# A two-layer encoder: x of the first MLP kept in DRAM tile by tile, 16 adaLN vectors computed in the space it leaves, and the squares and splits of the projection put in another order

## The chip, the cores and the metric

The kernel runs on one core of a Trainium2 chip. The metric is device time in microseconds (us). Three runs of the kernel before took 2743.26, 2744.90 and 2745.24 us; the median is 2744.9.

The engines have short names in the profile: PE is TensorE (matrix products), PEld its loads of the stationary operand, DVE is VectorE, ACT is ScalarE, POOL is GpSimd, and SPq is the queue on which SyncE issues transfers. A few transfers are issued from ACT's queue.

## The reference

All in float32, for one sequence of 1024 positions with 1024 features:

```python
cond = silu(c)
for i in range(2):
    mod = cond @ ada_w[i] + ada_b[i]                # 6 x 1024 numbers
    sh1, sc1, g1, sh2, sc2, g2 = split(mod, 6)
    h = rmsnorm(x, norm1_g[i]) * (1 + sc1) + sh1
    y = gqa_attention(h, ...) if i == 0 else chunked_gmlp(h, ...)
    x = x + g1 * y
    h = rmsnorm(x, norm2_g[i]) * (1 + sc2) + sh2
    x = x + g2 * (square(relu(h @ mlp_w_in[i])) @ mlp_w_out[i])
```

Layer 0 mixes with attention (16 heads, 4 key-value heads, QK norm and rotary positions), layer 1 with a gated unit of 3072 channels (gMLP). The MLPs have 4096 hidden features. An adaLN "vector" below is 128 of the 12 x 1024 numbers in `mod`: a tile of 128 x 1024 weights, each row multiplied by `cond` and summed. There are 96 of them. They are named (layer, j, k): j from 0 to 5 says which of shift, scale and gate, k from 0 to 7 which 128 features.

## The kernel before

x is kept transposed, as 16 tiles of 128 features by 512 positions: `x[hf][k]`, hf the half of the positions, k the block of features. Products are made in float32 precision from pairs: an operand is split into a rounded part `hi` (a cast on ACT) and a remainder `lo` (a subtraction, mostly on DVE; `split`, L285, and the last lines of each `prep`), and three matmuls hi·hi, hi·lo, lo·hi stand for one. The large products use one level of Winograd's scheme: seven products of half-size blocks in place of eight, named "1" to "7", with sums and differences of blocks ahead of them and of results behind them.

The stages in order, with their part of the profiled span: the projection to q, k and v (0 to about 205 us), attention, the output projection of attention (`wo_mm`, to 679), the first product of the first MLP (`winograd`, 112 units of 12 matmuls, 679 to 1004.6), its second product (`Out`, 112 units, to 1334), the values of the gMLP (`wino_v`), its other half (`winograd`, 84 units), its output product (`Out`, 84 units, 1854 to 2105), and the two products of the second MLP, to the end. `Out` reads the hidden activations from DRAM, where the first product has put them as ready-made forms: `load_f` (L1035) loads a form, `split_f` splits it (L287, L288), `prep` splits a weight block (L1057, L1058), `take` and `add` (L1089) add a result times the gate to x. `spread` makes the forms (L1141 to L1144), and SP stores them (L1145, L1146).

Between the products run hooks, called after each unit `i`: `at(i)` in the first product, `at_out(i)` in the second. They put the work of a norm, of a store or of a vector at a chosen unit. The numbers at the end of the file (HB, MO, MG and others) are these places.

Vectors are made in four ways and places. For those that the projection needs, `first_h` calls `mod_load`. `Slabs` makes 32 on POOL during attention. `mods(n)` takes the next n of the list `pending` (48 at the start) and is called in the projection, at the end of attention and in the output projection. The last 16 of the list, (1, 3, k) and (1, 5, k), are left for two later places: 12 are made in the second product of the first MLP, one at every third unit from unit 14 (`MO = (14, 3, 1)`), 4 in the output product of the gMLP, one at every fourth unit from unit 16 (`MG = (16, 4, 1)`). `mod_load` loads 128 x 1024 weights (L141), multiplies and sums on DVE (L145, followed by a short read of the accumulator) and adds the bias (L148). In both places the condition vector is loaded anew, spread over 128 partitions (`load_cond`, L134), and SiLU is applied to it (L137). These tiles come from a part of memory with the tag "c", four tiles of 128 x 1024, which `cut(4)` sets up 6 units before the first vector.

x stays in its 16 tiles (tag "x") through the whole first MLP. For the gMLP it is spilled: `spill` (L1279) stores each half in DRAM, since the gMLP needs the tiles, and `load_xs` (L1525) brings it back in four portions in the output product.

The order of work on each engine and queue is not that of the text alone. A planner takes the instructions in the order of the text, with the waits that their data and their tiles give, and lets a later instruction pass an earlier one when it reckons that the later one can start first. `pin` forbids this for one instruction: it stays behind everything that the text has before it on its engine. The multiplies of `mod_load` are pinned, and so is the SiLU (L137). The resulting order of each engine is fixed when the program is built; nothing is reordered while it runs, and a queue whose next transfer must wait holds back all that are behind it.

In the projection, `qkv_w(cb, kp, eng)` loads two tiles of weights and splits them: the casts on ACT (L498), the remainders on `eng` (L499), which is POOL (`G`) or DVE (`V`). `SquareSum.add` squares a tile on ACT (L231) and adds it to a running sum on DVE (L235). `norm_rstd` makes the norm's factor of it: a small product for the row sums (L244), a root, and a product that spreads the factor over the partitions (L255).

## Time and profile before

| | |
|---|---|
| median of three runs | 2744.9 us |
| time of the profiled execution | 2744.76 us |
| its span, first to last instruction | 2742.9 us |
| mean granted clock of TensorE | 0.984 |
| PE busy | 96% of the span, 12804 matmuls |
| DVE busy | 83%, 3191 instructions |
| ACT busy | 53%, 2598 instructions |
| POOL busy | 39%, 716 instructions |
| DMA | 427.52 MB, 156 GB/s on average |

A busy PE is not a PE at its peak: matmuls overlap, so the durations of single ones add up to more than the time that they take, and at a lower granted clock PE is busy and slow. How many matmuls fall into a stretch of time says more than its busy share. In rows of a timeline, a bracket with an arrow at the end gives the idle time of the engine ahead of the instruction and what ended it. The view of waits gives, for each pair of a waiting line and a releasing line, the total, the number and the longest wait.

### The profile page before, as it was taken

The page shows a single profiled execution, that of the slowest core. Times are in us where ns is not written, and L with a number is a line of the kernel's source. Part 1 is how long each engine was busy: PE and PEld are TensorE (multiplying, and loading weights), DVE is VectorE, ACT ScalarE, POOL GpSimd, SP SyncE. Part 2 cuts the span into 40 slices and gives each one's busy share as a digit, 9 for nine tenths or more (in the row PEclk, how much of TensorE's full clock was granted, in tenths as well). Part 3 has the DMA queues.
Part 4 walks back from the last instruction along what each step waited for, and adds up shares of the span by engine and source line. Part 5 has one row for each costly group of instructions (what it writes and reads, how often), then busy time and mean ns, then how long its engine had stood idle before and what let it go on. Part 6 is the DMA issues. An engine that isn't in the chain of part 4 may idle for free. (4 is left out here: it accounts for less than half of the span.)

```text
span 2742.9 us, 37309 instructions
## 1 busy us (share of the span) xinstructions
PE 2642.3 (96%) x12804; PEld 2184.9 (80%) x12804; DVE 2275.4 (83%) x3191; ACT 1454.5 (53%) x2598; POOL 1063.8 (39%) x716
## 2 busy tenths in 40 slices
PE   7889999999899999999999999999989999999999
PEld 5668999887688887777778888887868688878877
DVE  7889888888887778998797777787998887789993
ACT  4448999964644455435443355444436554554442
POOL 2448777534300024451543255556541400034520
PEclk9999999999999999999999999999999999999999
DMA  7241111225164458826244345558642364478462
GB/s 263 71 138 47 62 55 55 80 95 182 66 210 151 160 205 313 293 81 206 79 134 131 108 166 180 181 189 315 234 131 66 111 205 149 162 260 287 142 203 70
DMA packets 200544, 427.52 MB, mean 156 GB/s; under 512 B 23137, under 2 KB 35425, under 8 KB 200354
## 3 DMA queue, kind: packets, MB, share of 16 engines
q1 hardware_dynamic: 173474, 387.37, 41.6%
q10 hardware_dynamic: 26880, 37.76, 3.7%
q8 instruction: 101, 1.65, 0.2%
q14 instruction: 89, 0.73, 0.1%
HBM read 306.56 MB, written 118.49 MB: 155 GB/s over the span
## 5 line engine op out<-in xcount | busy, mean ns | idle before, releaser
L1074 PE MATMUL out<-t,s 128*128 128x512 f32 x1232 | 487.0, 396 | 14.3 <-DVE t L288 14.3
L1073 PE MATMUL out<-t,s 128*128 128x512 f32 x1232 | 487.0, 396 | 6.8 <-ACT t L287 6.8
L1075 PE MATMUL out<-t,s 128*128 128x512 f32 x1232 | 485.8, 395 | 6.0 <-DVE s L1058 5.7
L415 PE MATMUL w<-t,s 128*128 128x512 f32 x1168 | 460.1, 395 | 0.5 <-ACT t L287 0.5
L416 PE MATMUL w<-t,s 128*128 128x512 f32 x1168 | 455.5, 391 | 1.5 <-DVE t L288 1.1
L417 PE MATMUL w<-t,s 128*128 128x512 f32 x1168 | 454.9, 389 | 0.9 <-DVE s L401 0.9
L288 DVE TENSOR_TENSOR t<-t,t 128x512 fp32r<-128x512 f32 x408 | 377.9, 940 | 28.7 <-ACT t L287 21.2
L287 ACT CAST t<-t 128x512 fp32r<-128x512 f32 x408 | 244.3, 617 | 157.9 <-DMA t<-hf 65.2
L400 ACT CAST s<-w 128x512 fp32r<-128x512 f32 x292 | 174.3, 619 | 229.7 <-PE w L417 164.1
L1074 PEld LDWEIGHTS out<-t,s 128*128 128x128 f32 x1232 | 234.9, 191 | 70.7 <-DVE t L288 21.3
L1073 PEld LDWEIGHTS out<-t,s 128*128 128x128 f32 x1232 | 234.4, 190 | 60.1 <-ACT t L287 11.0
L1075 PEld LDWEIGHTS out<-t,s 128*128 128x128 f32 x1232 | 234.8, 191 | 59.3 <-DVE s L1058 11.1
L401 DVE TENSOR_TENSOR s<-w,s 128x512 fp32r<-128x512 f32 x292 | 227.9, 789 | 59.0 <-ACT s L400 55.4
L1044 POOL TENSOR_TENSOR w<-w,t 128x512 f32<-128x512 f32 x32 | 53.0, 1658 | 557.2 <-DMA t<-in_wm_dram 279.3
L416 PEld LDWEIGHTS w<-t,s 128*128 128x128 f32 x1168 | 219.4, 188 | 51.0 <-DVE t L288 6.7
L415 PEld LDWEIGHTS w<-t,s 128*128 128x128 f32 x1168 | 219.2, 188 | 49.6 <-issue 3.4
L417 PEld LDWEIGHTS w<-t,s 128*128 128x128 f32 x1168 | 219.3, 188 | 46.4 <-DVE s L401 1.3
L1058 DVE TENSOR_TENSOR s<-t,s 128x512 fp32r<-128x512 f32 x240 | 212.2, 886 | 49.2 <-ACT s L1057 46.4
L1057 ACT CAST s<-t 128x512 fp32r<-128x512 f32 x240 | 147.6, 620 | 188.7 <-PE out L1075 115.6
L860 DVE TENSOR_TENSOR t<-t,t 128x512 fp32r<-128x512 f32 x256 | 164.3, 683 | 20.9 <-ACT t L854 20.9
L837 DVE TENSOR_REDUCE mx<-s 128x1 f32<-128x1024 f32 x128 | 156.6, 1224 | 23.7 <-PE s L834 22.4
L870 PE MATMUL o<-t,t 128*128 128x256 f32 x1024 | 163.7, 293 | 0.0
(247 smaller groups left out, 5438.1 us busy)
## 6 DMA issues: line engine op xcount, KB each, us to landing
t<-hf SPq DMA_DIRECT2D x320, 256.0 KB, 4.5
hf<-c SPq DMA_DIRECT2D x156, 256.0 KB, 2.1
w<-in_wi_dram SPq DMA_DIRECT2D x64, 512.0 KB, 4.3
hf<-c ACTq DMA_DIRECT2D x96, 256.0 KB, 2.0
c<-in_ada_dram SPq DMA_DIRECT2D x36, 512.0 KB, 4.7
w<-in_adan_dram SPq DMA_DIRECT2D x32, 512.0 KB, 3.3
t<-in_wm_dram SPq DMA_DIRECT2D x64, 256.0 KB, 5.3
wf<-w SPq DMA_DIRECT2D x64, 256.0 KB, 3.3
```

Source lines behind the costliest of these rows:

```text
L287: S.copy(hi, src)
L288: (eng or V).tensor_tensor(lo, src, f32(hi), ALU.subtract)
L400: S.copy(hi, src)
L401: V.tensor_tensor(lo, src, f32(hi), ALU.subtract)
L415: T.matmul(ps, hi[:, a], th, start=kt == 0, stop=False)
L416: T.matmul(ps, hi[:, a], tl, start=False, stop=False)
L417: T.matmul(ps, lo[:, a], th, start=False, stop=kt == 3)
L860: pin(V.tensor_tensor(lo, pt, f32(hi), ALU.subtract))
L1058: V.tensor_tensor(lo, src, f32(hi), ALU.subtract)
L1073: T.matmul(ps, hi[:, a], th, start=begin and kt == 0, stop=False)
L1074: T.matmul(ps, hi[:, a], tl, start=False, stop=False)
L1075: T.matmul(ps, lo[:, a], th, start=False, stop=end and kt == 3)
```

## The change

1. **x of the first MLP through DRAM.** In the first product, at units 14 to 29 (HB + 12 and on), `spill` stores the 16 tiles of x in DRAM, one per unit. In the second product `load_xs` brings them back in four portions of four tiles: before the first unit, and at units 2, 6 and 10, as the gMLP does in its output product. `spill` takes a list of tiles now, and `xd`, `spill`, `load_xs` and the table of places XL have moved ahead of `mlp`. The gMLP's own spill stays.
2. **The last 16 vectors in the space left.** A new class, `Halves`, makes them in the first product of the first MLP out of free x tiles of 128 x 512: at unit 30 the condition vector is loaded as two halves, at unit 34 SiLU is applied to each and the weights of two vectors are loaded, as two halves each, and from unit 42 on, at every fourth unit (MX = 4), a vector is made by two multiplies with sums, one per half, while the next is loaded. The sums of both halves stay in a small tile, and when 8 vectors are done two short instructions add the halves and the bias for all 8 (before, one short instruction per vector). Neither the multiplies nor the SiLU is pinned.
3. **Vectors leave the second products.** The calls of `mods`, `load_cond` and `silu_cond` in `at_out` of the MLP and of the gMLP are gone. `cut(4)` is made at unit 8 in both (CUT = 8); it was at 8 in the MLPs and at 10 in the gMLP.
4. **The projection.** Three calls of `qkv_w` make their remainders on DVE in place of POOL (six subtractions), and the squares and sums of the second half of x, so far all eight in one loop, are added in three portions: tiles 0 to 2, 3 to 5, and 6 to 7, at three places.

```diff
--- before.py
+++ after.py
@@ -128,13 +128,6 @@
     ng = const.tile([P, 2, 2, KT], F32, name="ng")
     amod = const.tile([P, 2, 2, KT], F32, name="amod")
     cond = []
-
-    def load_cond(tile_):
-        cond[:] = [tile_]
-        nc.sync.dma_start(tile_, t["cond"].broadcast_to([P, D]))
-
-    def silu_cond():
-        pin(S.activation(cond[0], cond[0], AF.Silu))
 
     def mod_load(layer, j, k, tag="w", late=True):
         raw = wide(tag)
@@ -691,16 +684,20 @@
 
         ps = banks(True)
         kk = k_split(kd)
-        qkv_w(2, 1, G)
+        qkv_w(2, 1, V)
         qkv_mm(2, 0, ps, hs)
         r1 = q_copies(pq)
+        for k in range(3):
+            sq1.add(xs1[k])
         rr = q_sums(r1)
-        qkv_w(2, 2, G)
+        qkv_w(2, 2, V)
         qkv_mm(2, 1, ps, hs)
+        for k in range(3, 6):
+            sq1.add(xs1[k])
         q_rope(0, 1, r1, rr, (0, 1))
-        for k in range(KT):
+        qkv_w(2, 3, V)
+        for k in range(6, KT):
             sq1.add(xs1[k])
-        qkv_w(2, 3, G)
         qkv_mm(2, 2, ps, hs)
         rb1 = norm_rstd(sq1, bank_x)
         q_rope(0, 1, r1, rr, (2, 3))
@@ -1151,6 +1148,57 @@
     def forms_dram(n):
         return [{q: dram.tile([P, 512], F32, name=nm("hf")) for q in OUT_FORMS} for _ in range(n)]
 
+
+    xd = [[dram.tile([P, 512], F32, name=nm("xd")) for _ in range(KT)] for _ in range(2)]
+
+    def spill(hf, ks=range(KT)):
+        for k in ks:
+            nc.sync.dma_start(xd[hf][k], x[hf][k])
+
+    def load_xs(hf, odd):
+        for k in range(odd, KT, 2):
+            x[hf][k] = xslot()
+            nc.sync.dma_start(x[hf][k], xd[hf][k])
+
+    XL = {-1: (0, 0), 2: (0, 1), 6: (1, 0), 10: (1, 1)}
+
+
+    class Halves:
+        def __init__(self, todo):
+            self.todo, self.raw, self.part = list(todo), [], {}
+
+        def start(self):
+            self.cond = [xslot(), xslot()]
+            for h in range(2):
+                nc.sync.dma_start(self.cond[h], t["cond"][:, h * 512 : (h + 1) * 512].broadcast_to([P, 512]))
+
+        def silu(self):
+            for h in range(2):
+                S.activation(self.cond[h], self.cond[h], AF.Silu)
+
+        def load(self):
+            if self.todo:
+                layer, j, k = self.todo.pop(0)
+                raw = [xslot(), xslot()]
+                for h in range(2):
+                    nc.sync.dma_start(raw[h], t["ada"][layer, j * KT + k][:, h * 512 : (h + 1) * 512])
+                self.raw.append((layer, j, k, raw))
+
+        def step(self):
+            if not self.raw:
+                return
+            layer, j, k, raw = self.raw.pop(0)
+            self.load()
+            if k == 0:
+                self.part[j] = small.tile([P, 2, KT], F32, tag="half", name=nm("half"), bufs=2)
+            part = self.part[j]
+            for h in range(2):
+                V.scalar_tensor_tensor(raw[h], raw[h], 1.0, self.cond[h], ALU.mult, ALU.mult,
+                                       accum_out=part[:, h, k : k + 1])
+            if k == KT - 1:
+                V.tensor_tensor(part[:, 0], part[:, 0], part[:, 1], ALU.add)
+                V.tensor_tensor(mod[:, layer, j], part[:, 0], adab[:, layer, j], ALU.add)
+
     def mlp(layer, f, sqB, done, hook):
         hidden = forms_dram(16)
         out_ = Out(t["wm"][layer], hidden, 4, mod[:, layer, 5])
@@ -1177,9 +1225,22 @@
 
         n = 16 * 7
         rest = []
+        halves = None if layer else Halves(pending)
 
         def at(i):
             more(f, RW, None)
+            if halves:
+                h = i - HB - 12
+                if 0 <= h < 2 * KT:
+                    spill(h // KT, (h % KT,))
+                elif h == 2 * KT:
+                    halves.start()
+                elif h == 2 * KT + 4:
+                    halves.silu()
+                    halves.load()
+                    halves.load()
+                elif h > 2 * KT + 8 and h % MX == 0:
+                    halves.step()
             if i == HB:
                 rest.append(norm_ss(sqB, bank_y))
             elif i == HB + 1:
@@ -1195,17 +1256,15 @@
             stores.pop(0)()
 
         def at_out(i):
-            if i == MO[0] - 6:
+            if i == CUT:
                 cut(4)
-                if pending:
-                    load_cond(cwide())
-            elif pending and i == MO[0] - 2:
-                silu_cond()
-            if len(pending) > 4 and i >= MO[0] and (i - MO[0]) % MO[1] < MO[2]:
-                mods(1, "c")
+            if halves and i in XL:
+                load_xs(*XL[i])
             if hook and i >= out_.n - out_.tail:
                 hook(i - out_.n + out_.tail)
 
+        if halves:
+            load_xs(*XL[-1])
         out_.run(at_out, done)
 
     wo_sums(1)
@@ -1270,13 +1329,8 @@
         else:
             pieces[ct] = ((2 * i + 1, 0, P),)
 
-    xd = [[dram.tile([P, 512], F32, name=nm("xd")) for _ in range(KT)] for _ in range(2)]
     vd = [[dram.tile([2, P, 2, 256], F32, name=nm("vd")) for _ in range(4)] for _ in range(6)]
     st = small.tile([P, 8, 6, 6], F32, tag="st", name="st", bufs=1)
-
-    def spill(hf):
-        for k in range(KT):
-            nc.sync.dma_start(xd[hf][k], x[hf][k])
 
     def wino_v(f, hook):
 
@@ -1519,22 +1573,11 @@
         upto(n + 9)
         while stores:
             stores.pop(0)()
-        def load_xs(hf, odd):
-            for k in range(odd, KT, 2):
-                x[hf][k] = xslot()
-                nc.sync.dma_start(x[hf][k], xd[hf][k])
-
-        load_xs(0, 0)
-        XL = {2: (0, 1), 6: (1, 0), 10: (1, 1)}
+        load_xs(*XL[-1])
 
         def at_out(i):
-            if i == MG[0] - 6:
+            if i == CUT:
                 cut(4)
-                load_cond(cwide())
-            elif pending and i == MG[0] - 2:
-                silu_cond()
-            if pending and i >= MG[0] and (i - MG[0]) % MG[1] < MG[2]:
-                mods(1, "c")
             if i in XL:
                 load_xs(*XL[i])
             if i >= out_.n - out_.tail:
@@ -1565,8 +1608,8 @@
 FA = 3
 LO = 3
 TG = ((0, 0), (1, 0), (1, 1), (0, 1))
-MO = (14, 3, 1)
-MG = (16, 4, 1)
+CUT = 8
+MX = 4
 LW = 5
 IG = 30
 SW = 3
```

## The prediction

> **What bounds the kernel now.** I read the page first, then the busy times by stage, then the waits of PE, the instruction groups of the two stages the change takes work from, and the order of SP's queue.
>
> ```profile
> span 2742.9 us, 37309 instructions
> PE 2642.3 (96%) x12804; PEld 2184.9 (80%) x12804; DVE 2275.4 (83%) x3191; ACT 1454.5 (53%) x2598; POOL 1063.8 (39%) x716
> ```
>
> Each of the 12804 matmuls must be issued, and PE is idle for only 100.6 us of the span. An edit can win what PE loses in pauses and at a reduced clock, and can lose by adding pauses. The profiled execution took 2744.76 us, 1.86 us more than its span and 0.14 us under the median of the three runs, 2744.9; the sum below is made against 2744.76 and needs no shift.
>
> The next view cuts the span into stretches: length, then busy time and count of each engine, the granted clock PEclk, DMA share and GB/s.
>
> ```profile
> 70.00:120.00 50.00, 39.47 (x164) 30.20 (x164) 38.94 (x68) 20.02 (x41) 27.20 (x18) 0.86 0.20 65
> 679.00:764.00 85.00, 75.16 (x294) 57.32 (x293) 72.32 (x97) 46.59 (x83) 37.74 (x24) 0.92 0.25 84
> 764.00:1004.60 240.60, 240.60 (x1063) 199.31 (x1062) 185.70 (x293) 122.63 (x210) 0.00 (x0) 1.00 0.51 180
> 1004.60:1044.00 39.40, 36.13 (x149) 28.53 (x148) 31.83 (x35) 21.10 (x38) 24.47 (x16) 0.96 0.72 259
> 1044.00:1199.00 155.00, 153.70 (x673) 125.49 (x672) 152.28 (x196) 65.12 (x114) 78.33 (x49) 1.00 0.70 244
> 1199.00:1254.00 55.00, 48.74 (x188) 37.28 (x187) 52.51 (x65) 24.91 (x45) 23.31 (x15) 0.91 0.47 154
> 1889.00:1994.00 105.00, 105.00 (x464) 86.95 (x464) 104.22 (x121) 48.47 (x85) 61.79 (x39) 1.00 0.76 273
> 1994.00:2054.00 60.00, 52.98 (x203) 40.84 (x201) 56.07 (x67) 25.54 (x46) 23.62 (x16) 0.89 0.40 126
> 2425.50:2480.00 54.50, 52.88 (x232) 42.78 (x231) 47.37 (x53) 29.76 (x54) 27.77 (x17) 1.00 0.79 289
> 2480.00:2610.00 130.00, 130.00 (x575) 107.67 (x574) 123.96 (x147) 59.13 (x105) 70.95 (x45) 1.00 0.60 198
> 2610.00:2742.90 132.90, 126.01 (x545) 102.86 (x544) 85.81 (x121) 42.34 (x74) 16.56 (x11) 0.99 0.41 139
> ```
>
> 679 to 1004.6 is the first product of the first MLP, 1004.6 to 1334 its second product, 1854 to 2105 the output product of the gMLP, 2425.5 to the end the second product of the last MLP. In 764:1004.6 PE never pauses: 240.6 us over 1063 matmuls is 0.2263 us each, the price without loss. At that price: 679:764 loses 18.5 us (85 less 294 x 0.2263); in the first MLP's second product the three stretches lose 5.7, 2.7 and 12.5; the gMLP's output product loses 14.1 in 1994:2054; the last product 2.0, nothing and 9.6. In each of the late losses VectorE (DVE) has just been full: 152.28 of 155 us in 1044:1199, 104.22 of 105 in 1889:1994.
>
> **The change, part by part.**
>
> **Vectors leave the two output products.** The groups of 1004.6:1334, then those of 1854:2105 (busy us, mean ns | idle before):
>
> ```profile
> L1089 DVE SCALAR_TENSOR_TENSOR x<-t,mod,x 128x512 f32<-128x512 f32 x16 | 18.9, 1192 | 0.0
> L145 DVE SCALAR_TENSOR_TENSOR c<-c,c 128x1024 f32<-128x1024 f32 x12 | 16.8, 1403 | 0.0
> L148 DVE TENSOR_TENSOR mod<-mod,adab 128x1 f32<-128x1 f32 x12 | 5.0, 414 | 0.0
> L145 DVE DVE_READ_ACCUMULATOR c<-c,c 128x1 f32 x12 | 0.9, 77 | 0.0
> ```
>
> ```profile
> L145 DVE SCALAR_TENSOR_TENSOR c<-c,c 128x1024 f32<-128x1024 f32 x4 | 6.7, 1667 | 0.0
> L148 DVE TENSOR_TENSOR mod<-mod,adab 128x1 f32<-128x1 f32 x4 | 1.6, 392 | 0.0
> ```
>
> In the first MLP's second product 12 vectors go: 16.8 + 5.0 + 0.9 = 22.7 us of DVE; in the gMLP's output product 4, 6.7 + 1.6 and a third of those 0.9, 8.6. Their 16 transfers, two loads of the condition vector and two SiLUs go from there too. What is late without them? SP's queue shows it, in order of time and then in its waits (total, times, longest):
>
> ```profile
> 1168.24 4.41 SPq L1035 DMA_DIRECT2D t<-hf  x3
> 1198.73 0.32 SPq L1279 DMA_DIRECT2D xd<-x  x1
> 1199.14 0.38 SPq L1035 DMA_DIRECT2D t<-hf  x1
> ```
>
> ```profile
> SPq L1279 <- DVE x L1089: 107.1, 16, 26.1
> ```
>
> The spill of x for the gMLP (L1279), which the program text has behind this product, stands inside it: the planner puts a transfer where it thinks the data are ready. DVE, behind by then, wrote x (L1089) late, SP stood still for 26.1 us at the longest, and the loads of activations behind it (L1035) started at 1199.14. PE paused there, as it had before, for other loads:
>
> ```profile
> 1202.49 0.50 PE L1073 MATMUL out<-t,s 128*128 128x512 f32 x1 [1.10 <-ACT t L287]
> ```
>
> ```profile
> 1031.67 0.51 PE L1073 MATMUL out<-t,s 128*128 128x512 f32 x1 [1.51 <-ACT t L287]
> 1033.00 0.51 PE L1074 MATMUL out<-t,s 128*128 128x512 f32 x1 [0.82 <-DVE t L288]
> ```
>
> So the 2.7 + 12.5 = 15.2 us lost after 1044 come from DVE's lag through that spill. The spill stays; the lag shrinks. Bounds: 0 (the spill waits anyway) and 15.2. The nearest row is the last product, the same 112 units without vectors, whose stores of the output wait for the same x: DVE is at 123.96 of 130 us and the stretch behind loses 9.6, of which 4 lie after the last matmul's start:
>
> ```profile
> 2738.82 0.39 PE L1075 MATMUL out<-t,s 128*128 128x512 f32 x1
> ```
>
> I take 15.2 - 5.6 = about **10 us**. The early 5.7 us, before the first vector, stay. For the gMLP's output product the bounds are 0 and 14.1; I take **4**, in proportion to the DVE time (8.6 against 22.7). Moving the cut from unit 10 to 8 there only renames free memory: nothing, or the wait for a tile if one is still in use.
>
> The clock belongs to this. With pauses of 1.51 and 0.82 us and matmuls between them, the next 5 us were granted 0.66:
>
> ```profile
> 1034.00:1039.00 5.00, 5.00 (x16) 3.91 (x15) 3.70 (x5) 2.38 (x5) 3.34 (x2) 0.66 1.04 394
> ```
>
> In the Trainium skill, "TensorE: Matmul & The Clock Gate", Part 1, the array falls to half rate after at least one idle window of about 3.4 us; by that rule pauses as short as these cost no clock, 1199:1254 would give back at most its idle 55 - 48.74 = 6.3 us, the 10 would be about 5 and the sum 5 us higher. The row shows a fall after shorter pauses, so I price it by the row.
>
> **The vectors in the first product.** Added: 32 multiply-and-sum over 128x512 with 32 accumulator reads and 4 short adds. The nearest price is that of L1089, one input in PSUM and no POOL beside it:
>
> ```profile
> L1089 DVE SCALAR_TENSOR_TENSOR x<-out,mod,x x124: 735/742/752, 1022.2 to 2739.2; 128x512 f32<-128x512 f32 x124
> ```
>
> At its median of 0.74 and the 0.08 of an accumulator read above that is 26 us. The text puts them at units 42 to 102, inside 764:1004.6, where DVE has 240.6 - 185.70 = 54.9 us free and POOL does nothing: hidden there. The cover is not certain. The multiplies are not pinned to the text's order, as those of before were, so the planner can move them ahead, as it moved the spill, into 679:764, where DVE is at 72.32 of 85 and PE already loses 18.5. Ends: 0 when all are covered, 26 when all are ahead of needed work; less than nothing is excluded, since nothing leaves DVE here. I take **4**, nearer to the covered end: a planner that fills gaps finds most of them in the longer stretch.
>
> The Trainium skill, "SBUF — State Buffer", Who interferes with whom, says that a DVE instruction with two SBUF inputs contends with a GpSimd instruction reading SBUF. The trace agrees: x<-t,mod,x takes 1192 ns on average beside POOL above, x<-out,mod,x, with one input in PSUM, 742.
>
> **x through DRAM.** Added on SP: 16 spills, 16 reloads, and 32 half loads plus 2 for the condition, in place of 16 and 2 of double size.
>
> ```profile
> c<-in_ada_dram SPq DMA_DIRECT2D x36, 512.0 KB, 4.7
> xd<-x SPq DMA_DIRECT2D x16, 256.0 KB, 2.0
> x<-xd SPq DMA_DIRECT2D x16, 256.0 KB, 5.5
> ```
>
> A transfer itself lies beside matmuls (DMA is at 0.51 in 764:1004.6), and reloads of 5.5 us have the whole of that stretch free for them: nothing, and if that is gone a reload holds an x add and, through it, DVE. The condition's halves wait for two x tiles that a spill has left, a half load for a tile that a multiply has read; behind them on SP stand the product's weights and the stores of the hidden forms, which wait for DVE at the same place. The gMLP's own spill waits for the reloads of the same buffers, long done: nothing. What can cost is order on SP: a spill moved ahead to where x is just being written makes the weight loads behind it wait, as L1279 did. Ends: 0, and the 12.5 us of 1199:1254, the one place where such a spill went wrong. I take **1**: these x are final before the stage begins, so few can meet an unfinished one. SiLU moves with its table load to ScalarE at 122.63 of 240.6 us: nothing.
>
> **The projection.** Six lo-splits go from POOL to DVE, and the squares of the second half of x are summed in three portions. DVE, POOL and PE in order of time:
>
> ```profile
> 72.94 1.29 DVE L499 TENSOR_TENSOR t<-c,t 128x512 fp32r<-128x512 f32 x2
> 82.44 2.67 DVE L605 TENSOR_TENSOR t<-t,t 128x512 fp32r<-128x512 f32 x4 [1.88 <-ACT t L604]
> 87.52 2.47 DVE L557 TENSOR_REDUCE qss<-t 128x8 f32<-128x512 f32 x4 [2.40 <-ACT t L556]
> 96.06 9.59 DVE L235 TENSOR_TENSOR t<-t,t 128x512 f32<-128x512 f32 x7
> ```
>
> ```profile
> 100.12 3.39 POOL L499 TENSOR_TENSOR t<-c,t 128x512 fp32r<-128x512 f32 x2
> ```
>
> ```profile
> 101.89 0.58 PE L510 MATMUL qkv<-t,t 128*128 128x512 f32 x1 [4.44 <-POOL t L499]
> 105.71 1.87 PE L244 MATMUL ss<-ones,t 128*128 128x1 f32 x8 [1.97 <-DVE t L235]
> 118.40 0.50 PE L509 MATMUL qkv<-s,t 128*128 128x512 f32 x1 [0.23 <-ACT t L268]
> ```
>
> PE waits 4.44 us for POOL's split and 1.97 for the row sum behind seven adds that take 9.59 us, 1.37 each, beside POOL. The first matmul on the new half starts at 118.40, 12.7 after that sum. Without POOL's splits an add costs what a DVE split costs, 1.29 / 2 = 0.65: seven adds and six splits are 8.4 us, and 1.88 + 2.40 of idle time (rows 82.44 and 87.52) can take some. Added to the 96.06 at which DVE now begins its adds, the last ends between 100.2 and 104.5, 5.4 to 1.2 us before 105.65. Ends: a gain of 10.5 (PE's loss there: its idle time in 70:120, 50 - 39.47), and a loss of 3.9, six DVE splits in front of the rest of the chain. I take **5**, the upper part of that 1.2 to 5.4, as the pause at 101.89 and the clock behind it (0.86 in 70:120) go with it.
>
> Sum: 2744.76 - 10 - 4 + 4 + 1 - 5 = 2730.76, **2731 us**; all costs at the ends taken alone: 2744.76 - 15.2 - 14.1 - 10.5 = 2705 and 2744.76 + 26 + 12.5 + 3.9 = 2787.
>
> **The rivals.**
>
> **The vectors arrive early and DVE's full stretch grows** (slower). Place: 679:764. Price: up to 26 us for multiplies and up to 12.5 for spills that hold weights, against the 4 + 1 in the sum: 2731 + 33.5 = 2764 at the worst. It decides when the cost passes the 10 + 4 + 5 = 19 us won elsewhere, that is when some 23 of the 32 multiplies stand in front of work that PE waits for. For it: 18.5 us already lost there, and the spill's place in SP's row. Against: DVE is idle for 12.7 of these 85 us, too, and the planner gives way to earlier work when both are ready.
>
> **The gain of the output products does not come** (no change). The spill L1279 and loads behind it remain, and other work fills DVE: in 2480:2610, without vectors, it is at 95%. Then only the projection's 5 and the costs of 5 are left: 2745. Against: with DVE that full there PE loses nothing in that stretch.
>
> **DVE becomes the bound in the projection.** The six splits come before the sums that PE waits for: instead of 5 won, 3.9 lost: 2740, at the edge of no change. For it: DVE is at 38.94 of 50 us in 70:120. Against: POOL slowed it there, and leaves.
>
> **How the numbers follow.** No change means within 0.2%, 5.5 us, about what a measurement can tell. The forecast, with its own range 2714 to 2739, 0.66; DVE in the projection 0.06, half of it faster and half no change; the gain that does not come 0.08; the early vectors 0.20. So faster 0.69, same 0.11, slower 0.20. The range reaches up into the early vectors, to 2757, and down to 2714, where both output products give nearly all they lose.
>
> **What would show it.** In the profile after: no L145 rows beyond the first product, DVE under 90% in the stretch that now reads 152.28 of 155, SP's wait at L1279 well under 26.1, the pause at 1202 gone and the clock 1.00 there; the sum of squares done by 104 us; and DVE rows of the halves mostly behind the first 85 us of the MLP. Wrong if these rows stand in those 85 us and the stage is longer than 325.6 us by over 15, or if L1279 still holds SP for 20 us, or if new x reloads or spills head SP's waits.

## The result, and the profile after

The changed kernel takes 2745.5 us (median of 20 runs, 2742.0 to 2752.3) against 2744.4 us for the kernel before (20 runs, 2740.7 to 2748.2): ratio 1.0005, 95% interval 0.9998 to 1.0012. Nothing was won. The forecast was 2731 us and faster.

The profiled execution of the changed kernel took 2751.21 us, 5.7 us over its own median, and the one of before 2744.76, 0.36 over its. So the two traces differ by 6.45 us, more than the medians do, and a length of one stage read from one trace is good to some 3 or 4 us: stages that the change does not touch differ by that much between the kernels below (the values product of the gMLP took 241.6 to 245.4 us, the attention 393.8 to 397.4).

Cut at the first matmul of each stage, in us:

| stage | before | after | difference | forecast |
|---|---|---|---|---|
| projection | 185.7 | 181.3 | -4.4 | -5 |
| attention | 396.3 | 396.3 | 0 | 0 |
| attention output | 97.0 | 99.5 | +2.5 | 0 |
| first MLP, first product | 325.7 | 343.1 | **+17.4** | +5 |
| first MLP, second product | 329.0 | 320.5 | -8.5 | -10 |
| gMLP, values | 242.4 | 245.4 | +3.0 | 0 |
| gMLP, u | 281.2 | 281.1 | -0.1 | 0 |
| gMLP, output product | 252.6 | 249.5 | -3.1 | -4 |
| last MLP, both products and what follows | 634.9 | 634.5 | -0.4 | 0 |

The three gains came, nearly as large as forecast. One stage gave all of it back. The page's first lines after, then the busy times by stretch (columns as before: stretch, length, busy time and count of PE, PEld, DVE, ACT, POOL, then PEclk, DMA share, GB/s), each stretch lying in its stage within some 3 us of where the one of before lay:

```profile
span 2749.4 us, 37427 instructions
PE 2639.9 (96%) x12804; PEld 2183.9 (79%) x12804; DVE 2269.4 (83%) x3217; ACT 1452.0 (53%) x2597; POOL 1050.8 (38%) x710
```

```profile
70.00:120.00 50.00, 42.57 (x188) 32.60 (x187) 42.42 (x81) 23.33 (x45) 20.01 (x12) 0.93 0.21 70
677.00:762.00 85.00, 62.62 (x219) 44.16 (x217) 80.08 (x145) 42.36 (x74) 31.71 (x20) 0.84 0.60 194
762.00:1020.00 258.00, 258.00 (x1137) 213.43 (x1138) 197.83 (x311) 131.62 (x224) 5.08 (x4) 1.00 0.53 181
1020.00:1060.00 40.00, 38.17 (x159) 30.56 (x158) 35.85 (x36) 21.39 (x39) 25.67 (x16) 0.96 0.76 277
1060.00:1215.00 155.00, 155.00 (x685) 128.40 (x684) 140.88 (x169) 66.97 (x119) 77.55 (x50) 1.00 0.61 204
1215.00:1270.00 55.00, 49.83 (x209) 39.24 (x209) 51.59 (x72) 23.68 (x43) 20.76 (x13) 0.97 0.47 163
1902.00:2007.00 105.00, 105.00 (x462) 86.89 (x461) 96.26 (x110) 46.48 (x82) 59.08 (x38) 1.00 0.69 243
2007.00:2067.00 60.00, 53.82 (x227) 42.54 (x226) 56.21 (x76) 26.43 (x49) 23.08 (x15) 0.97 0.42 132
```

At the forecast's price of a matmul without loss, 0.2263 us, 677:762 loses 85 - 219 x 0.2263 = 35.4 us, where before it lost 18.5. The rest of the stage is without loss, as before (258.00 of 258). The second product loses 4.0, nothing and 7.7, where before it lost 5.7, 2.7 and 12.5; the gMLP's output product 8.6 where it lost 14.1, behind a stretch in which VectorE (DVE) is at 96.26 of 105 us (before 104.22). PE's and DVE's totals on the page hardly move, so the time is a matter of when, not of how much.

In 677:762 DVE is now at 80.08 of 85 us with 145 instructions, against 72.32 with 97. The new ones are the multiplies with their reads, 26.57 us in this stretch. All 32 ran between 665.5 and 745 us, not at units 42 to 102 where the text has them (line's own view: shortest, median, longest in ns, then first and last start):

```profile
L1196 DVE SCALAR_TENSOR_TENSOR x<-x,x x32: 665/686/1785, 665.5 to 743.3; 128x512 f32<-128x512 f32 x32
L1196 DVE DVE_READ_ACCUMULATOR x<-x,x x32: 76/80/89, 666.1 to 745.0; 128x1 f32 x32
```

What PE waited for in that stretch, before and then after (total, times, longest):

```profile
PE w L415 <- ACT t L287: 4.4, 3, 2.6
PE w L417 <- DVE t L288: 4.1, 3, 1.6
```

```profile
PE w L408 <- ACT t L280: 12.1, 4, 9.1
PE w L409 <- DVE t L281: 5.6, 5, 1.7
PE w L410 <- DVE t L281: 4.2, 4, 2.4
```

The longest of these, 9.1 us, reads as a chain when the engines are set in order of time. PE, then the same 9 us as a stretch, then ACT and SP:

```profile
692.35 0.79 PE L408 MATMUL w<-t,t 128*128 128x512 f32 x1 [9.08 <-ACT t L280]
```

```profile
683.28:692.35 9.07, 0.00 (x0) 0.00 (x0) 9.07 (x17) 2.25 (x5) 3.22 (x2) 0.75 0.53 158
```

```profile
687.75 0.63 ACT L224 ACTIVATE t<-x 128x512 f32<-128x512 f32 x1 [4.93 <-DVE x L793]
691.68 1.28 ACT L280 CAST t<-t 128x512 fp32r<-128x512 f32 x2 [2.31 <-DMA t<-in_wi_dram]
```

```profile
681.29 6.12 SPq L1184 DMA_DIRECT2D x<-in_ada_dram  x3
687.50 1.81 SPq L360 DMA_DIRECT2D t<-in_wi_dram  x4
```

```profile
673.87 3.81 SPq L367 DMA_DIRECT2D t<-in_wi_dram  x8
```

While PE did nothing for 9.07 us, DVE was busy for all 9.07. ScalarE stood 4.93 us for an update of x that DVE (L793) was late with, and then 2.31 us for a weight load. That load (L360, a small weight tile of forms 1 or 2) was issued at 687.50, behind half loads (L1184) that stood in SP's queue from 681.29. Before, all eight such loads had gone out in one row from 673.87. The chain has two possible roots, DVE's time and SP's order, and this trace alone does not part them.

### The profile page after: what moved, and what is told of

Read it like the earlier page. It is cut to its first block, busy times and chain, and to the rows that moved or that the text cites. A ratio compares the mean times of both kernels' runs of the same rounds, so it can differ in the third digit from the quotient of the medians.

```text
span 2749.4 us, 37427 instructions
## 1 busy us (share of the span) xinstructions
PE 2639.9 (96%) x12804; PEld 2183.9 (79%) x12804; DVE 2269.4 (83%) x3217; ACT 1452.0 (53%) x2597; POOL 1050.8 (38%) x710
## 5 line engine op out<-in xcount | busy, mean ns | idle before, releaser
L1071 PEld LDWEIGHTS out<-t,s 128*128 128x128 f32 x1232 | 233.5, 190 | 65.9 <-DVE t L281 17.4
```

The source lines that it names most:

```text
L1071: T.matmul(ps, hi[:, a], tl, start=False, stop=False)
```

## The experiments

Theory V: the early multiplies take DVE's time when the matmuls need its splits. Rival Q: spills and half loads stand ahead of weight loads on SP, and DVE's full stretch is a consequence. Each run compares with the kernel before on the same chip (2743.5 to 2745.3 us there). The stage lengths are again between first matmuls.

**The multiplies held in the text's place.** (Code is shortened in all cuts; `...` stands for what is left out.)

```
-                V.scalar_tensor_tensor(raw[h], ..., accum_out=part[:, h, k : k + 1])
+                pin(V.scalar_tensor_tensor(raw[h], ..., accum_out=part[:, h, k : k + 1]))
```

> The kernel after, with one edit: the 32 multiplies of the halves may not be moved ahead of the instructions that the text has in front of them. In the planned order they then stand at units 42 to 102, while 16 spills, the two condition loads and 12 half loads still stand on SP ahead of the weight loads of forms 1 and 2 (the small ones, t from in_wi). Theory V (the early multiplies, 29.0 us of VectorE's time, fill it when the matmuls need its splits): the first product of the first MLP goes from 343.1 back to 326 to 330 us, the whole to about 2731. Theory Q (SP's order: spills and half loads hold up the weight loads behind them, and VectorE's full stretch is a consequence): the product stays at 340 to 343, the whole at 2742 to 2746. Half from each: product about 335, whole about 2737.

2728.7 us, ratio 0.9951 (0.9931 to 0.997). First product 324.9 us. Its multiplies, and the stretch:

```profile
L1196 DVE SCALAR_TENSOR_TENSOR x<-x,x x32: 679/686/691, 811.7 to 979.5; 128x512 f32<-128x512 f32 x32
```

```profile
677.00:762.00 85.00, 73.63 (x297) 56.41 (x296) 72.20 (x99) 51.43 (x90) 37.34 (x24) 0.94 0.40 131
762.00:1003.00 241.00, 241.00 (x1065) 199.54 (x1064) 203.31 (x360) 122.41 (x208) 0.00 (x0) 1.00 0.65 218
```

They now lie between 811 and 980 us, where DVE is at 203.31 of 241 us (before 185.70 of 240.6) and PE loses nothing at all. Covered multiplies cost zero, as the forecast said of the covered end. This one line of the change separates its failure from its success. SP's early spills and the first half loads are still there, and the small weight loads are nearly as late as in the changed kernel, 7.7 us after the product's first matmul (there 10.4), so Q in its full form falls:

```profile
685.30 3.25 SPq L360 DMA_DIRECT2D t<-in_wi_dram  x7
```

**The multiplies short, in their early place.** Each sums 64 of its 512 columns, so the 16 vectors come out wrong.

```
-                V.scalar_tensor_tensor(raw[h], raw[h], 1.0, self.cond[h], ...
+                V.scalar_tensor_tensor(raw[h][:, :64], raw[h][:, :64], 1.0, self.cond[h][:, :64], ...
```

> The kernel after with each of the 32 multiplies over 64 columns in place of 512 (7/8 of each vector's sum is left out, so the output is another). All transfers stay, early, and the multiplies too, but most of the 29.0 us that these take of VectorE between 665 and 745 us is gone. Theory V: first product 326 to 331 us, whole about 2731. Theory Q: product 338 to 343, whole 2741 to 2746, with ScalarE still waiting for a weight load near the product's 15th microsecond (2.3 us in the kernel after, PE idle for 9).

2734.8 us, ratio 0.9969 (0.996 to 0.9979); first product 330.4 us, in V's range, the whole between the two. The multiplies and their reads still take 14.26 us of DVE here, half of the 29.0, so the run is less of a "none" than its expectation took it for. (The row is of L1196 alone: stretch, length, DVE's time and count, clock, DMA share, GB/s.)

```profile
660.00:745.00 85.00, 14.26 (x64) 0.90 0.67 227
```

One thing did not become shorter: PE's longest pause, 8.6 us, again at the first small weight block, whose loads are issued 9.4 us after the first matmul:

```profile
PE w L408 <- ACT t L280: 10.4, 2, 8.6
```

**x through DRAM alone, and then the loads without the multiplies.** In both, the 16 vectors hold only their bias.

```
                 elif h == 2 * KT:
-                    halves.start()
-                ...
-                elif h > 2 * KT + 8 and h % MX == 0:
-                    halves.step()
```

> The kernel after without the halves: no condition loads, half loads, SiLUs and multiplies (the 16 vectors hold only their bias, so the output is another); x still goes through DRAM tile by tile and comes back, all early. It is the cost of x through DRAM alone. Theory V: product 325 to 328 us, as before the change; whole about 2729. Theory Q, if the spills hold the weight loads: product 333 or more, whole 2736 or more; if the half loads are what holds them, 328 or less here and 340 in the kernel with only the multiplies moved back.

2730.7 us, ratio 0.9961 (0.9946 to 0.9975); first product 324.4. Spills and reloads cost the first product nothing, though the small weight loads are issued 7.6 us after its first matmul here.

The second of the two keeps all loads and takes only the multiplies out:

```
-            ...
-            part = self.part[j]
-            for h in range(2):
-                V.scalar_tensor_tensor(raw[h], raw[h], 1.0, self.cond[h], ...)
```

> The kernel after without its 32 multiplies (the 16 vectors hold only their bias, so the output is another). The spills, the condition loads, the two SiLUs, all half loads and the reloads stay, as early as before: 15 half loads and most spills stand on SP ahead of the first weight loads of forms 1 and 2, only that no half load waits for a multiply to free its tile. If the order on SP costs by itself (the issue time of what stands ahead, the DMA's load): first product 329 to 332 us, as with short multiplies, whole about 2734. If the order costs only through tiles that VectorE is late to free: 323 to 326, as without halves (324.4), whole 2728 to 2731; then the 6 us between short multiplies and none are VectorE's as well.

2730.5 us, ratio 0.9956 (0.9941 to 0.9971); first product 326.6, just above the range for "only through tiles that VectorE is late to free" and below that for "order by itself". SP's queue has much the same order as in the changed kernel, and the DMA engines are as busy (0.65 in 677:762, there 0.60); six half loads now pass in 2.83 us and the weight loads follow at 680.33, not 687.50:

```profile
677.40 2.83 SPq L1184 DMA_DIRECT2D x<-in_ada_dram  x6
680.33 2.10 SPq L360 DMA_DIRECT2D t<-in_wi_dram  x4
```

These runs give a price for the multiplies in this stretch. With loads and no multiplies the whole takes 2730.5 us; with 14.3 us of multiplies 2734.8; with 29.0 us 2745.5. The first 14.3 us cost 4.3, the next 14.7 cost 10.7: 0.30 and then 0.73 us for each us of DVE. (By the stage lengths, 326.6, 330.4 and 343.1, it is 3.8 and 12.7.) The first 4.3 is within the noise of the two runs, whose intervals overlap. That DVE's slack went first is one reading; the other is that the short multiplies cost by the 8.6 us pause, which is 5.1 to 5.3 us where they are held or left out, and so through SP. The step from the short to the full ones is clear by either: ScalarE waits 2.3 us in all for small weight loads with the full ones and 3.9 with the short, the longest pause is 0.5 us longer, and yet the stage grows by 12.7. That part is the multiplies' time on DVE, with what they hold up on POOL.

**The weight loads issued by ScalarE.**

```
-                nc.sync.dma_start(passing[(q, p)], wsrc(2 * p)[:, i : i + 4])
+                way[0].dma_start(passing[(q, p)], wsrc(2 * p)[:, i : i + 4])   # ScalarE in the first MLP
```

> The kernel after with one edit: in the first MLP the weight loads of forms 1 and 2 are issued by ScalarE in place of SP, so spills and half loads no longer stand ahead of them, while the multiplies stay early. It splits the 17.4 us that the first product lost. In the kernel with short multiplies the product still took 330.4 us, 6 more than without halves (324.4), with ScalarE waiting 3.4 us for such a load. If SP's order is worth those 6 us and VectorE's time the rest (12.7, 343.1 less 330.4): product about 337 us, whole about 2739. If VectorE's time alone sets it and the late loads are covered by it: 341 to 344, whole 2743 to 2746. If the late loads were the most of it: under 333, whole under 2735. A wait of ScalarE at the loads it now issues would be seen in its own queue.

2744.7 us, ratio 0.9997 (0.9987 to 1.0006); first product 339.7 us. The time says VectorE alone, the stage lies between the cases. But the loads did not become early:

```profile
L361 ACTq DMA_DIRECT2D t<-in_wi_dram x8: 334/362/508, 685.9 to 711.1; - x8
```

```profile
ACT t L281 <- DMA t<-in_wi_dram: 4.2, 1, 4.2
```

ScalarE issues them in its own order, behind its waits for DVE, at 685.9 to 711.1, and still waits 4.2 us for one. The edit moved the late loads to another late queue, so it does not part the two roots. What parts them is the multiplies held, where the loads are late too and nothing is lost. SP's order adds to the loss only through tiles that the early multiplies free late; how much of the 17 us goes that way is not shown; by the short multiplies it is some 6 at the most (330.4 less the 324.4 without halves).

**The transfers held.**

```
-            nc.sync.dma_start(xd[hf][k], x[hf][k])
+            ld = nc.sync.dma_start(xd[hf][k], x[hf][k])
+            if len(ks) == 1:                  # the spills of the first MLP
+                pin(ld)
-                nc.sync.dma_start(self.cond[h], ...)
+                pin(nc.sync.dma_start(self.cond[h], ...))
-                    nc.sync.dma_start(raw[h], t["ada"][...]...)
+                    pin(nc.sync.dma_start(raw[h], t["ada"][...]...))
```

> The kernel after, with the spills, the condition loads and the half loads kept behind what the text has in front of them (units 14 to 30 for the spills, then the loads), the multiplies free but tied to their late data: planned at units 40 to 100. SP's weight loads of forms 1 and 2 stand ahead of all of them again. Both theories: product 325 to 330 us, whole about 2730. What it tells is the rest: if it is below the kernel with only the multiplies held by more than 3 us, SP's order has a price of its own of that size; if above, the late spills (beside a fuller DMA and SP's stores) have one.

2726.1 us, ratio 0.9944 (0.9928 to 0.996); first product 325.3. Late data made the multiplies late (792 to 959 us) without a hold on them. Compared with the kernel that holds the multiplies it is 2.6 us faster, with overlapping intervals. The traces show a difference of that size in the attention output: 98 to 100 us in all six kernels with spills moved ahead into it (99.3 with the multiplies held, 99.5 in the changed kernel, 99.8 with spills only), 96 to 97 in all eight without (96.5 here). So spills moved ahead into the attention output cost some 2.6 us there, by the means. That is what is left of Q without early multiplies.

**Multiplies and transfers held, then the reloads too.** The first kernel has the holds on the multiplies and on the transfers as above, the second in `load_xs` also

```
+            if late:                          # the reloads of x in the first MLP
+                pin(ld)
```

> The kernel with the moved transfers held (2726.1 us) and the 32 multiplies held too. The multiplies come early nowhere in either, so both theories expect no difference beyond 2 us: first product 324 to 326 us, whole 2724 to 2729. More than 4 us either way would say that a multiply's exact place in the long full stretch counts, against the forecast's zero for a covered multiply.

2725.4 us, ratio 0.9931 (0.9912 to 0.9949); first product 323.9. This is the fastest version run: on the same chip the kernel before took 2745.3. A multiply's exact place within the stretch without loss does not matter.

> The same with the 16 reloads of x held to the text's order as well: four before the second product, the rest at its units 2, 6 and 10 in place of far ahead. The forecast costs a reload at nothing while it has the first product's stretch for it, and says that a late one holds an addition to x and, through it, VectorE. Reloads land some 5.5 us after issue (median before) and the first addition to x comes in the product's first 20 us. If 5.5 us is early enough: second product 319 to 322 as with early reloads, whole 2724 to 2729. If not: VectorE waits for x at those additions, product 324 or more, whole 2730 or more.

2730.9 us, ratio 0.9949 (0.9935 to 0.9964); the second product took 324.9 us against 320.3. The cover of the reloads was real: with them at the product's start it loses time, in its first 40 us. Early reloads, then late ones (in the second the product begins 2.8 us earlier; its 40 us from 993.2 on read the same, 140 matmuls, clock 0.91, DMA share 0.89):

```profile
996.00:1036.00 40.00, 38.34 (x167) 30.76 (x166) 37.39 (x39) 23.04 (x42) 26.17 (x16) 1.00 0.74 265
```

```profile
996.00:1036.00 40.00, 35.57 (x140) 27.63 (x140) 32.09 (x32) 17.64 (x33) 24.65 (x16) 0.91 0.90 332
```

```profile
PE out L1070 <- ACT t L280: 3.7, 1, 3.7
```

The expected way is not what the trace shows: no addition to x heads DVE's waits. The DMA engines are at 0.90 in place of 0.74 while the product's first loads arrive, and PE waits 3.7 us in one piece for a split. That the reloads slowed those loads is likely and was not tried alone.

**The gains by themselves.** The vectors (but for their bias) and x's way through DRAM both left out:

```
-                if 0 <= h < 2 * KT:
-                    spill(h // KT, (h % KT,))
-                elif h == 2 * KT:
-                    halves.start()
-                ...
-            load_xs(*XL[-1])
```

> The kernel after without the halves and without x's way through DRAM in the first MLP: the 16 vectors hold only their bias (the output is another), x stays in its memory. It shows the gain of the two output products with nothing given back. If the 8.5 us and 3.1 us won there come from the vectors' leaving: second product of the first MLP 319 to 322 us, output product of the gMLP 249 to 252, first product 324 to 327, whole 2728 to 2731. If the second product's gain came from x being loaded anew instead, that product goes back to 326 or more and the whole to 2736.

2728.2 us, ratio 0.9949 (0.9934 to 0.9964); second product 319.6, gMLP's output product 251.0, first product 324.4. The second product's gain is the vectors' leaving, not the reloading of x.

The projection's edit alone on the kernel before:

```
-        qkv_w(2, 1, G)
+        qkv_w(2, 1, V)
         ...
+        for k in range(3):
+            sq1.add(xs1[k])
```

> The kernel before with the projection's edit alone (three splits on VectorE, the squares in three portions). Forecast: 5 us less in the projection (185.7 to about 181), nothing elsewhere: whole 2739 to 2741. Rival, the 4.4 us seen in the changed kernel are spent again by the attention stages, which start earlier but wait for loads: projection 181, whole 2743 to 2745.

2738.3 us, ratio 0.9986 (0.9976 to 0.9996), a gain of 1 to 7 us with 3.8 in the middle. In its trace the projection takes 183.2 us, not the 181 expected; over all traces it took 180.4 to 183.2 with this edit and 185.2 to 185.7 without. The attention took 395.4 us (before 396.3), so the gain is not spent again there. In the changed kernel the sum of squares comes at 102.31 us (before 105.71) and the new half's first matmul at 113.05 (before 118.40); the split that PE waited 4.44 us for now holds it 0.52:

```profile
99.41 0.50 PE L503 MATMUL qkv<-t,t 128*128 128x512 f32 x1 [0.52 <-DVE t L492]
102.31 1.05 PE L237 MATMUL ss<-ones,t 128*128 128x1 f32 x8 [0.54 <-DVE t L228]
113.05 0.50 PE L502 MATMUL qkv<-s,t 128*128 128x512 f32 x1 [1.37 <-ACT t L261]
```

**The gMLP's spill late.** Its edit on the kernel before, and on the one with the transfers held:

```
-            nc.sync.dma_start(xd[hf][k], x[hf][k])
+            pin(nc.sync.dma_start(xd[hf][k], x[hf][k]))
```

> The kernel before with one edit: the spill of x for the gMLP may not be moved ahead, so it stands on SP in its place of the text, behind the first MLP's second product, not inside it. Theory L (the forecast's: VectorE's lag costs PE through SP, which stands still for the spill with the activations' loads behind it): the second product goes from 329.0 to 317 to 321 us, whole about 2734 to 2736. Theory F (VectorE is late with the splits themselves; SP's stand hides nothing that is needed): 327 to 329 us, whole 2742 or more. In the changed kernel SP still stood at the spill for up to 27.2 us and the product was 8.5 us shorter, which speaks for F.

2747.9 us, ratio 1.0019 (1.0009 to 1.003); second product 328.0 against 329.0. Theory L falls. The whole is 4.4 us slower, not faster; its values product took 245.2 us (before 242.4), but the changed kernel's took 245.4 without this hold, so where the 4.4 come from stays open. The loss behind the full stretch stays, and DVE is as full:

```profile
1043.00:1198.00 155.00, 153.33 (x670) 124.73 (x668) 153.02 (x198) 64.38 (x113) 78.46 (x48) 1.00 0.73 256
1198.00:1253.00 55.00, 47.51 (x195) 37.29 (x194) 52.78 (x65) 24.17 (x44) 23.05 (x15) 0.94 0.48 149
```

The spills run from 1303.5 us on (before from 1198.7), and the pause that the forecast put down to them is still there, as long as before:

```profile
1199.45 0.49 PE L1073 MATMUL out<-t,s 128*128 128x512 f32 x1 [1.10 <-ACT t L287]
```

> The kernel with the moved transfers held (2726.1 us), and the gMLP's spill held as well. Theory L: the second product of the first MLP, 319.4 there, falls to 313 to 316, whole about 2721. Theory F: 318 to 320 and the whole within 2 us of 2726. A later spill could also free the x buffers later for the gMLP's value product: then that grows from 242.4.

2728.4 us, ratio 0.9951 (0.9936 to 0.9965); second product 321.9 against 319.4. Theory F again.

## Why the prediction was wrong

**The step that failed** is "a planner that fills gaps finds most of them in the longer stretch", from which the 32 multiplies were costed at 4. (The 1 for x through DRAM had another reason, that "these x are final before the stage begins".) The ends were right: 0 when covered (first product 324.9 us with them held), 26 when ahead of needed work. But all 32 stood ahead, and stage by stage the two terms came to 17.4 in the first product and 2.5 in the attention output, 19.9 in place of 5. With that number the forecast is 2731 + 14.9 = 2746, half a microsecond above the median measured; so close a fit is partly luck, with stages that are good to 3 or 4 us. By medians the same two terms are the changed kernel less the one with multiplies and transfers held, 2745.5 - 2725.4 = 20.1. The planner places an instruction when its data are ready, not where an engine is idle for longer: the spills were moved ahead of the matmuls of the stage, as L1279 had been in the trace of before, they freed x tiles, the half loads followed, and with their data there the multiplies did too. The row that the forecast quoted for the spill held for the whole chain behind it.

**The rival of the early vectors** named the place, 679:764, and the point from which it decides, 19 us. It came in at 19.9, on that point, and so ended at no change and not slower. It was given 0.20. "DVE is idle for 12.7 of these 85 us, too", said against it, was worth little: of 29.0 us added, the first half cost some 0.30 us each, within the noise, and the second 0.73.

**The second product, -10:** -8.5, and -9.4 with nothing else in the way (329.0 to 319.6); with early reloads it took 319.4 to 323.3 us in every kernel without vectors there, 328.0 to 329.7 with them. The size was right and the mechanism not. The forecast led the loss from DVE's lag through SP's stand at the spill to late loads. In the changed kernel SP stands as long as before, 27.2 us at the longest (before 26.1), while the product is shorter:

```profile
SPq L1156 <- DVE x L1086: 105.0, 15, 27.2
```

And holding that spill back won nothing. What changed is DVE itself, 140.88 of 155 us in place of 152.28 (91%, a little above the forecast's 90). PE's pauses were waits for splits, 10.8 us of them in the product before and 8.0 after. The way to the pause at 1202.49 goes through ScalarE: it stood 7.42 us for a late addition to x, to square it, then 0.90 us for another, and the cast (L287) that PE needed stood behind. The trace of before has the first:

```profile
1198.74 0.63 ACT L231 ACTIVATE t<-x 128x512 f32<-128x512 f32 x1 [7.42 <-DVE x L1089]
```

The forecast took the row in front of the pause for its cause; one edit of the kernel before would have told. That it is DVE's time which was won back, and not the vectors' transfers (the DMA share there went from 0.70 to 0.61), is argued: no run parts the two.

The pauses in that place were not gone, either: PE's idle time in 1215:1270 is 5.17 us (before 6.26), the granted clock 0.97 (0.91). So of the 12.5 - 7.7 = 4.8 us won there 1.1 are idle time, and the rest goes with the clock. In the Trainium skill, "TensorE: Matmul & The Clock Gate", Part 1, the clock falls after an idle window of some 3.4 us, by which the gain would have been about half; the gain measured does not bear that out for pauses this short.

**The gMLP's output product, -4:** -3.1. Without vectors there it took 249.0 to 251.4 us over all kernels, with them 252.6 to 254.9. **The projection, -5:** -4.4, alone 3.8 with the interval above; its rival, DVE as the bound, is out.

**x through DRAM, +1:** nothing in the first product (324.4 us with spills and reloads alone), some 2.6 in the attention output, a place that the forecast did not price: it took few spills to meet an unfinished x, since x is final before the stage begins, and 14 of the 16 (from 585.8 us on) moved ahead of the stage. Its sentence that a reload costs if its cover is gone holds (4.6 us), by another way than the one named.

**The forecast's own test** was well put: "wrong if these rows stand in those 85 us and the stage is longer than 325.6 us by over 15". They do, and it is, by 17.4 over the stage of before. The sign at the spill came as well: it still holds SP for over 20 us, and this one said nothing about the time.

## What to carry to other kernels

When work is costed at nothing because it lies under a long full stretch, ask what keeps it there. Where a planner orders the work by readiness, follow its inputs back: if its loads, and the buffers that they wait for, can be early, the work will be early too, and the one stretch that must be priced is the one in which they become ready. Holding 32 instructions in the text's order was worth 15 to 17 us here, and holding their transfers as well 20.

A queue's long wait in front of a pause of PE is not yet its cause; look whether the wait is as long where the pause is gone.

## What the hardware showed that was not expected

Beside POOL's work a DVE multiply with two SBUF inputs took up to 1785 ns; the same 32 with POOL idle took 679 to 691. That the two get in each other's way was in the forecast; that the size of the multiply then hardly matters was not. Over 64 columns it took 194 ns at the shortest, and 1.3 us in the worst cases. One of these beside POOL's instruction, DVE and then POOL in order of time:

```profile
680.36 1.28 DVE L1196 SCALAR_TENSOR_TENSOR x<-x,x 128x64 f32<-128x64 f32 x1
```

```profile
679.92 1.64 POOL L390 TENSOR_TENSOR w<-w 128x512 f32<-128x512 f32 x1 [0.63 <-DVE s L394]
```

POOL's instruction ends at 681.56, the multiply at 681.64. All eight short multiplies that took over 0.7 us end 0.08 us after an instruction of POOL, and all seven full ones that took over 1.6 us end 0.55 us after one: a multiply that starts behind POOL's instruction waits for its end. The forecast's 1192 ns for x<-t,mod,x was a mean of the same two kinds: the 16 had a median of 741 ns and a longest of 1776. The Trainium skill, "SBUF — State Buffer", Who interferes with whom, has a DVE instruction with two SBUF inputs contend with a GpSimd instruction that reads SBUF, and calls the shared pair of ports an exclusive lock; these rows agree.

The granted clock fell to a half without a long pause: within 6 us PE waited 1.66, 1.75 and 1.20 us, with matmuls between, and from the third wait on it got 0.50 for 3.4 us. PE's rows and that stretch, in the changed kernel:

```profile
715.12 0.50 PE L408 MATMUL w<-t,s 128*128 128x512 f32 x1 [1.66 <-ACT t L280]
717.37 0.50 PE L409 MATMUL w<-t,s 128*128 128x512 f32 x1 [1.75 <-DVE t L281]
719.78 0.80 PE L410 MATMUL w<-t,t 128*128 128x512 f32 x1 [1.20 <-DVE t L281]
```

```profile
719.10:722.50 3.40, 2.71 (x6) 2.15 (x7) 3.40 (x9) 1.67 (x3) 0.79 (x1) 0.50 1.00 351
```
